# Rotation phasors made by ScalarE's sine beside the first down product, and a reshaped 1/rms step, in a two-layer FoX + S5 trunk

## The chip, the cores and the metric

The kernel runs on one core of a Trainium2 chip. The metric is the device time of one execution, in microseconds (us).

## The reference

Two layers, each a token mixer and a dense SwiGLU, on 1024 tokens of width 1024 in float32; every mixer and every SwiGLU stands between two rmsnorms.

```python
for i in range(DEPTH):                       # 2 layers
    h = rmsnorm(x, mix_pre_gain[i])
    m = fox_mixer(...) if i == 0 else s5_mixer(...)
    x = x + rmsnorm(m, mix_post_gain[i])
    h = rmsnorm(x, ffn_pre_gain[i])
    x = x + rmsnorm((silu(h @ w_gate) * (h @ w_up)) @ w_down, ffn_post_gain[i])

# s5_mixer: 64 groups of 64 complex states, 16 channels each
u = h @ w_in
a = exp((lam_re + 1j * lam_im) * dt)         # the pole of each state
bb = (a - 1) / lam * b
x_t = a * x_(t-1) + bb @ u_t                 # scan over the tokens
y = gelu(Re(c @ x_t) + d * u)
return (y * sigmoid(y @ w_glu)) @ w_out
```

`rmsnorm` is `x * rsqrt(mean(x^2) + eps) * gain`. What the change works on is the unit phasor of a pole, `exp(1j * angle * n)` for n = 0 to 127 tokens: the S5 stage turns its states by it.

## The kernel before, in words

Every product runs on TensorE in pieces of 128x512 from operands cut into a high and a low part (`split`: a cast on ScalarE, a subtraction on VectorE), three matmuls for one. SBUF is handed out as numbered pages: a ring such as `s5w0` or `s5w1` is one or more pages, and a tile's first write waits until the page's last user is done. The code fixes the order in which each engine gets its work through a scheduler, and all loads and stores go through SyncE's queue (SP) one behind the other.

The stages are, by the trace: first norm and start, attention (to about 600 us), its output product, `gate_up` 0 (775 to 1230), `down` 0 (1230 to 1415), the S5 mixer and its products (to 1806), `gate_up` 1 (to 2216), `down` 1, and the tail of the last norms.

`gate_up` has 11 periods p of 14 steps s. A step is 12 matmuls of 128x512. Beside the products of layer 0 a generator, `s5_params`, prepares the S5 mixer; the caller lets it go on by one piece after the steps (p, s) that `when` names: (5, 9, 12) in most periods. It begins with `s5_small` (poles, their powers, power tables), and then goes through 8 chunks of the states, one a period, the last after step 5 of the last period. In a chunk, before the change:

- GpSimd (POOL) makes `kg` and `cp` (L1183 to L1187); `kg` lies in ring `s5w1`. `cp_d` is stored (L1197).
- After step 5, TensorE multiplies `cp` into 16 small products `pk` (L1201); ScalarE copies them to `KT`, stored by L1207; POOL makes `bp` by L1237 to L1239, the lines of `prod`, which VectorE uses too.
- After step 9, `finish` transposes `bp` on TensorE (L1168, 8 matmuls of 128x128), copies it to `T` in ring `s5w1` (L1170) and stores it (`T_d`, L1171).
- Between steps 9 and 12, `s5_rot` multiplies two tables of phasors (`R1`: steps of 8, `R2`: steps of 1 or of 128) into the chunk's 128x1024 phasors `rot`, by six VectorE operations of 128x512 (`prod` again), in rings `s5w0` and `s5w1`. After step 12 they are stored (`rot_d`, L1228), and the next chunk's `kg` begins.

In the last period the steps are (5, 7, 9, 11). `down` multiplies the stored activations by the down weights in three phases of 11 steps; loads of both come through SP, and the casts for them run on ScalarE and VectorE. `rstd` (L301 to L304) makes 1/rms of 128 tokens from a sum of squares by a square root on ScalarE, a reciprocal and one refinement step on 128x1 values; `norm` applies it on VectorE (L314) or on POOL (L311, a multiplication by the gain, then L312, a scaling), and `to_fm` transposes the result on TensorE (L322).

Of the kernel before, what the change touches and what calls it, by code (L numbers as in the profile page):

```python
# [20 lines left out]
NF = FF // P  # L21
# [4 lines left out]
MAGIC = 1.5 * 2.0 ** 23  # L26
# [132 lines left out]
class Trunk:  # L159
# [129 lines left out]
    def rstd(self, src, junk, part=None, out=None):  # L289

        nc = self.nc
        V = nc.vector
        ss = self.small("ss")
        s = slice(0 if part is None else 512, D)
        nc.scalar.activation(junk[:, s], src[:, s], AF.Square, accum_out=ss)
        if part is not None:
            V.tensor_add(ss, ss, part)
        rt = self.small("rt")
        self.sqrt = nc.scalar.activation(rt, ss, AF.Sqrt, bias=self.eps, scale=1.0 / D)
        v, t, rr = self.small("vv"), self.small("tt"), self.small("rr") if out is None else out  # L300
        V.tensor_scalar(v, ss, -0.5 / D, -0.5 * EPS, op0=ALU.mult, op1=ALU.add)  # L301
        V.reciprocal(rr, rt)
        V.scalar_tensor_tensor(t, rr, v, rr, op0=ALU.mult, op1=ALU.mult)
        V.scalar_tensor_tensor(rr, t, 1.5, rr, op0=ALU.add, op1=ALU.mult)  # L304
        return rr

    def norm(self, src, gain, out, pool=False):
        nc = self.nc
        rr = self.rstd(src, out)
        if pool:  # L310
            nc.gpsimd.tensor_mul(out, src, gain)  # L311
            self.poolop = nc.gpsimd.tensor_scalar(out, out, rr, 1.0, op0=ALU.mult, op1=ALU.mult)  # L312
        else:
            nc.vector.scalar_tensor_tensor(out, src, rr, gain, op0=ALU.mult, op1=ALU.mult)  # L314
# [608 lines left out]

    def down(self, finish, begin=lambda tb, m: None, extra=0, last=3):

# [3 lines left out]
        nc, R = self.nc, self.R  # L929
# [11 lines left out]
        for ph in range(3):  # L941
            for p in range(n):
                g = self.take()
                if ph:
                    self.take()
                w = self.take()
                for tb in range(4):
                    mm(X[tb], g, w, 0, tb, p == ph == 0)
                    mm(Y[tb], g, w, 1, tb, p == 0)
                if ph == 0 and p < extra:  # L950
                    self.take()
            with self.tc.high_priority(AHEAD):
                for tb in range(4):
# [50 lines left out]
    def s5_small(self):  # L1004
# [48 lines left out]
        V.memset(hpi, math.pi / 2)  # L1053
        ang, n, r, sn, cs = (w[:, 8 + 3 * i:11 + 3 * i] for i in range(5))
        used[0] = 23
        for i, k in enumerate((1.0, 8.0, 128.0)):
            V.tensor_scalar_mul(ang[:, i], th, k)
        C1 = 6.28125
        C2 = math.floor((2 * math.pi - C1) * 2 ** 20) / 2 ** 20
        C3 = 2 * math.pi - C1 - C2  # L1060
        ts(n, ang, 1.0 / (2 * math.pi), MAGIC, op0=ALU.mult, op1=ALU.add)
        V.tensor_scalar_sub(n, n, MAGIC)
        for k, (x, o) in zip((C1, C2, C3), ((ang, r), (r, r), (r, r))):
            stt(o, n, -k, x, op0=ALU.mult, op1=ALU.add)
        ts(r, r, 3.1415925, -3.1415925, op0=ALU.min, op1=ALU.max)
        nc.scalar.activation(sn, r, AF.Sin)
        nc.scalar.activation(cs, r, AF.Abs)
        nc.scalar.activation(cs, cs, AF.Sin, bias=hpi, scale=-1.0)
        pw = R("pw", (P, 2, 9, 32))
        Pre, Pim = pw[:, 0], pw[:, 1]  # L1070
        self.R1, R2 = R("R1", (P, 2, 32, 16)), R("R2", (P, 1024))
        self.bs = R2[:, 512:640].rearrange("p (q g m) -> p q g m", q=4, g=2)
# [3 lines left out]
        nc.sync.dma_start(self.g5, bass.AP(tensor=v.tensor, offset=v.offset, ap=[[1, P], [P, 8]]))  # L1076
        self.R2 = R2[:, 0:512].rearrange("p (i a n) -> p i a n", i=2, n=8)
        R1, R2 = (x.rearrange("p i a n -> p i n a") for x in (self.R1, self.R2))
        for X in (pw, R1, R2):
            V.memset(X[:, 0, 0], 1.0)  # L1080
            V.memset(X[:, 1, 0], 0.0)
        tt(Pre[:, 1], mag, cs[:, 0], op=ALU.mult)
        tt(Pim[:, 1], mag, sn[:, 0], op=ALU.mult)
        for X, i in ((R1, 1), (R2, 2)):
            V.tensor_copy(X[:, 0, 1], cs[:, i])
            V.tensor_copy(X[:, 1, 1], sn[:, i])
        kk = R("s5t2", (P, 2, 16, 32))
# [12 lines left out]
        yield  # L1100
        powers(R1, 15)
        yield
        powers(R2, 7)

# [24 lines left out]
    def s5_params(self):  # L1129
# [84 lines left out]
        finish(7, bp)  # L1214
        yield from self.s5_rot(7)

    def s5_rot(self, ch):

        R, sh, V = self.R, (P, 4, 8, 16), self.nc.vector
        pr = slice(4 * ch, 4 * ch + 4)  # L1220
        rot, k = R("s5w0", sh[:1] + (2,) + sh[1:]), R("s5w1", sh[:1] + (2,) + sh[1:])
        e1 = [self.R1[:, i, pr, None, :].to_broadcast(sh) for i in range(2)]
        e2 = [self.R2[:, i, pr, :, None].to_broadcast(sh) for i in range(2)]
        self.prod(V, rot[:, 0], e1[0], e2[0], e1[1], e2[1], ALU.subtract, k[:, 0])
        self.prod(V, rot[:, 1], e1[0], e2[1], e1[1], e2[0], ALU.add, k[:, 1])
        yield
        with self.tc.issue_after(self.sp.ins):
            self.nc.sync.dma_start(self.rot_d[ch], rot.rearrange("p i a b c -> p (i a b c)"))  # L1228

# [268 lines left out]
def trunk(ctx: ExitStack, tc: tile.TileContext, A, out):  # L1498
# [179 lines left out]
```

## Time and profile before

| | |
|---|---|
| three runs | 2443.24, 2446.89 (the median), 2448.79 us |
| the profiled execution | 2441.36 us by its own time, span 2439.6 us |
| TensorE busy | 2362.7 us, 97% of the span |
| VectorE busy | 1747.5 us, 72% |
| ScalarE busy | 1175.4 us, 48% |
| POOL busy | 472.3 us, 19% |
| DMA | 318.25 MB, 130 GB/s in the mean |

The span is the time from the first to the last recorded instruction; the profiled execution's own time is 1.8 us longer, and it is 5.5 us under the median of the three. "Busy" counts the time in which an engine has an instruction at work. TensorE is busy but for 77 us, so what the profile lists as TensorE's waits is all that a change of order can win, except where the granted clock falls.

### The profile page before, as it was taken

The numbers are of one execution on the slowest core, as the hardware profiler recorded it, in microseconds if no ns is written. First come the engines' busy times: TensorE is split into PE (matmuls) and PEld (weight loads), VectorE is DVE, ScalarE is ACT, GpSimd is POOL, SyncE is SP. The second block draws the span as 40 slices with busy tenths as digits, with TensorE's granted clock in tenths as the row PEclk, the third lists the DMA queues.
The fourth block names the chain that finished last, engine by engine and source line by source line (L and its number), as shares of the span: only waits on it lengthen the run. The fifth ranks groups of instructions, "written<-read, shape, count | busy, mean of one in ns | idle before, by whom it ended". The sixth has DMA issues, their size and how long they took to land.

```text
span 2439.6 us, 31625 instructions
## 1 busy us (share of the span) xinstructions
PE 2362.7 (97%) x11683; PEld 1938.0 (79%) x11683; DVE 1747.5 (72%) x2746; ACT 1175.4 (48%) x1997; POOL 472.3 (19%) x427
## 2 busy tenths in 40 slices
PE   7999999999999999999999999999999999999998
PEld 5777778777777887777788888988878888888886
DVE  6867776677678968788678686763785656555867
ACT  5766676667646333433344363332453333333334
POOL 3222222223300035555530001320000000000003
PEclk9999999999999999999999999999999999999999
DMA  4221111121343433434498652443424233237874
GB/s 129 64 61 46 51 52 61 53 61 53 92 151 106 128 105 130 137 123 140 167 321 305 220 179 78 131 156 107 129 93 132 94 112 108 91 117 255 285 236 160
DMA packets 252428, 318.25 MB, mean 130 GB/s; under 512 B 34224, under 2 KB 179936, under 8 KB 252272
## 3 DMA queue, kind: packets, MB, share of 16 engines
q1 hardware_dynamic: 252272, 316.23, 40.1%
q8 instruction: 91, 1.49, 0.3%
q14 instruction: 65, 0.53, 0.1%
HBM read 238.46 MB, written 77.72 MB: 130 GB/s over the span
## 4 chain that ended last, share of the span: by engine, by line
PE 72%; DVE 12%; ACT 6%; POOL 4%; issue 3%; DMA 2%; SPq 0%; DVEq 0%; POOLq 0%; ACTq 0%
PE ps L837 27%; PE ps L939 15%; PE ps L272 7%; PE ps L274 7%; PE ps L273 7%; PE ps L584 2%; PE ps L603 2%; POOL s5w L1238 1%; DVE ps L551 1%; POOL s5w L1239 1%; DMA raw<-in_ffn_w_gate_dram 1%; ACT wh L253 1%; POOL s5w L1237 1%; PE ps L548 1%; PE ps L547 1%
## 5 line engine op out<-in xcount | busy, mean ns | idle before, releaser
L837 PE MATMUL ps<-B,ah 128*128 128x512 f32 x1056 | 327.3, 391 | 0.3 <-ACT B L89 0.2
L939 PE MATMUL ps<-wdh,gl 128*128 128x512 f32 x616 | 240.5, 391 | 1.8 <-DVE gl L254 1.8
L939 PE MATMUL ps<-wdl,gh 128*128 128x512 f32 x616 | 240.8, 391 | 0.6 <-DVE wdl L254 0.6
L939 PE MATMUL ps<-wdh,gh 128*128 128x512 f32 x616 | 240.3, 390 | 0.0
L837 PEld LDWEIGHTS ps<-B,ah 128*128 128x128 f32 x1056 | 197.6, 188 | 42.1 <-ACT B L89 1.2
L837 PE MATMUL ps<-ops,ah 128*128 128x512 f32 x704 | 220.1, 394 | 0.0
L272 PE MATMUL ps<-hT,wh 128*128 128x512 f32 x512 | 207.7, 406 | 1.2 <-DVE pt L425 0.6
L837 PE MATMUL ps<-B,al 128*128 128x512 f32 x528 | 205.5, 389 | 0.0
L273 PE MATMUL ps<-hT,wh 128*128 128x512 f32 x512 | 204.1, 399 | 0.0
L274 PE MATMUL ps<-hT,wl 128*128 128x512 f32 x512 | 202.5, 395 | 0.0
L253 ACT CAST gh<-gr 128x1024 fp32r<-128x1024 f32 (+1 forms) x78 | 81.2, 1041 | 206.0 <-PE ps L939 172.7
L588 DVE TENSOR_TENSOR ptl<-ps,pth 128x512 fp32r<-128x512 f32 x192 | 106.3, 554 | 78.7 <-ACT pth L587 73.7
L254 DVE TENSOR_TENSOR gl<-gr,gh 128x1024 fp32r<-128x1024 f32 (+1 forms) x78 | 98.3, 1262 | 88.2 <-ACT gh L253 88.2
L837 PEld LDWEIGHTS ps<-ops,ah 128*128 128x128 f32 x704 | 132.4, 189 | 29.3 <-issue 1.7
L1629 POOL TENSOR_TENSOR y<-m,s 128x512 f32<-128x512 f32 x4 | 7.2, 1796 | 764.8 <-DVE wdl L254 759.9
L543 POOL TENSOR_TENSOR An<-An,cmask 128x128 f32<-128x128 f32 x128 | 80.5, 630 | 367.2 <-DVE mx L551 332.7
L808 DVE TENSOR_TENSOR al<-raw,ah 128x1024 fp32r<-128x1024 f32 x88 | 111.8, 1272 | 44.8 <-ACT ah L807 44.7
L807 ACT CAST ah<-raw 128x1024 fp32r<-128x1024 f32 x88 | 92.3, 1050 | 99.2 <-PE ps L837 96.4
L837 PE MATMUL ps<-ops,al 128*128 128x512 f32 x352 | 137.8, 391 | 0.0
L939 PEld LDWEIGHTS ps<-wdh,gl 128*128 128x128 f32 x616 | 116.1, 188 | 26.4 <-DVE gl L254 2.4
L939 PEld LDWEIGHTS ps<-wdl,gh 128*128 128x128 f32 x616 | 116.1, 188 | 25.2 <-DVE wdl L254 1.3
L939 PEld LDWEIGHTS ps<-wdh,gh 128*128 128x128 f32 x616 | 116.0, 188 | 24.6 <-DVE s L862 0.5
(353 smaller groups left out, 5919.6 us busy)
## 6 DMA issues: line engine op xcount, KB each, us to landing
raw<-in_ffn_w_down_dram SPq DMA_DIRECT2D x98, 512.0 KB, 5.1
gr<-g_d SPq DMA_DIRECT2D x76, 512.0 KB, 4.3
raw<-in_ffn_w_gate_dram SPq DMA_DIRECT2D x44, 512.0 KB, 4.1
raw<-in_ffn_w_up_dram SPq DMA_DIRECT2D x44, 512.0 KB, 4.1
g_d<-s SPq DMA_DIRECT2D x66, 256.0 KB, 2.1
raw<-in_fox_w_in_dram SPq DMA_DIRECT2D x32, 512.0 KB, 4.2
g_d<-up SPq DMA_DIRECT2D x22, 512.0 KB, 2.6
g_d<-up SPq DMA_DIRECT2D x44, 256.0 KB, 2.4
```

The source lines that it names most:

```text
L253: self.nc.scalar.copy(h, src)
L254: self.lsub.tensor_sub(l, src, f32(h))
L272: mm(ps, lh, rh, start=start, stop=False)
L273: mm(ps, lh, rl, start=False, stop=False)
L274: mm(ps, ll, rh, start=False, stop=stop)
L543: nc.gpsimd.tensor_add(An[h][:, qs], An[h][:, qs], self.cmask)
L584: nc.tensor.transpose(p2[:, i], p[:, (g + i) * P:(g + i + 1) * P], self.ident)
L588: nc.vector.tensor_sub(dl, p2[:, 0:n], f32(dh))
L807: nc.scalar.copy(h, src)
L808: V.tensor_sub(l, src, f32(h))
L837: nc.tensor.matmul(bank, x[:, k], y, start=start and k == i == 0, stop=True, skip_group_check=True)
L939: nc.tensor.matmul(bank, x[:, j, t], y[:, j], start=start and i == 0, stop=True, skip_group_check=True)
```

## The change

It has three parts.

1. `rstd`: the two refinement operations took two SBUF tensors each (`scalar_tensor_tensor`). Now each takes one tensor, and the second value enters as a per-partition scalar (`tensor_scalar`).
2. The first norm: for token blocks 1 and 3 the gain multiplication on POOL is issued ahead of `rstd`, whose squares now go to a page of their own (`j`); the ring of `y` has one more page.
3. The phasors: the tables `R1` and `R2` go. `s5_small` makes a table `ph` of phases instead (sums of two phases, each brought back into one turn by subtraction). `s5_rot` leaves `s5_params`; it is run beside `down` 0, one half of a chunk after each of 8 steps in phase 0 and 8 in phase 2. A chunk is now one VectorE addition (128x512), an absolute value on ScalarE twice (128x512), once more and then the sine on both halves (128x1024), and the store. `s5_params` is called after steps (5, 12) in most periods, the last among them, and after 12 also in the second.

```diff
-        V.scalar_tensor_tensor(t, rr, v, rr, op0=ALU.mult, op1=ALU.mult)
-        V.scalar_tensor_tensor(rr, t, 1.5, rr, op0=ALU.add, op1=ALU.mult)
+        V.tensor_scalar(t, v, rr, rr, op0=ALU.mult, op1=ALU.mult)
+        V.tensor_scalar(rr, t, 1.5, rr, op0=ALU.add, op1=ALU.mult)
...
-    def norm(self, src, gain, out, pool=False):
+    def norm(self, src, gain, out, pool=False, junk=None):
+
         nc = self.nc
-        rr = self.rstd(src, out)
+        if junk is not None:
+            nc.gpsimd.tensor_mul(out, src, gain)
+        rr = self.rstd(src, out if junk is None else junk)
         if pool:
-            nc.gpsimd.tensor_mul(out, src, gain)
+            if junk is None:
+                nc.gpsimd.tensor_mul(out, src, gain)
...
-    def down(self, finish, begin=lambda tb, m: None, extra=0, last=3):
+    def down(self, finish, begin=lambda tb, m: None, beside=iter(()), steps=((),) * 3, extra=0, last=3):
...
+                if p in steps[ph]:
+                    next(beside, None)
...
-        nc.scalar.activation(sn, r, AF.Sin)
-        nc.scalar.activation(cs, r, AF.Abs)
+        nc.scalar.activation(sn, r[:, 0], AF.Sin)
+        nc.scalar.activation(cs, r[:, 0], AF.Abs)
...
-        powers(R1, 15)
-        yield
-        powers(R2, 7)
+        n, N = 1, kk.rearrange("p i n a -> p (i n a)").rearrange("p (n m) -> p n m", m=64)
+        while n < 15:
+            c_ = min(n, 15 - n)
+            x, q = X[:, n + 1:n + 1 + c_], N[:, :c_]
+            tt(x, X[:, 1:1 + c_], X[:, n:n + 1].to_broadcast([P, c_, 64]), op=ALU.add)
+            ts(q, x, 1.0 / (2 * math.pi), MAGIC, op0=ALU.mult, op1=ALU.add)
+            V.tensor_scalar_sub(q, q, MAGIC)
+            stt(x, q, -C1, x, op0=ALU.mult, op1=ALU.add)
+            stt(x, q, C1 - 2 * math.pi, x, op0=ALU.mult, op1=ALU.add)
+            ts(x, x, LIM, -LIM, op0=ALU.min, op1=ALU.max)
+            n += c_
+            if n == 8:
+                yield
...
                 finish(ch - 1, bp)
-                yield from self.s5_rot(ch - 1)
...
-        yield from self.s5_rot(7)
-
-    def s5_rot(self, ch):
...
+    def s5_rot(self):
+
+
+        act, sh = self.nc.scalar.activation, (P, 4, 8, 16)
+        mpi, hpi = self.mpi[:, 0:1], self.mpi[:, 1:2]
+        for ch in range(8):
+            pr = slice(4 * ch, 4 * ch + 4)
+            x, y = self.R("rx", sh), self.R("ry", (P, 2) + sh[1:])
+            with self.tc.high_priority(-150):
+                self.nc.vector.tensor_tensor(x, self.ph[:, 0, pr, None, :].to_broadcast(sh),
+                                             self.ph[:, 1, pr, 0:8, None].to_broadcast(sh), op=ALU.add)
+                act(y[:, 0], x, AF.Abs)
+                act(y[:, 1], x, AF.Abs, bias=hpi)
+            yield
+            with self.tc.high_priority(-150):
+                act(y, y, AF.Abs, bias=mpi)
+                act(y, y, AF.Sin, bias=hpi)
+            with self.tc.issue_after(self.sp.ins):
+                self.nc.sync.dma_start(self.rot_d[ch], y.rearrange("p i a b c -> p (i a b c)"))
+            yield
...
-            T.norm(xs[tb], g0[0], ys[tb], tb % 2 == 1)
+            T.norm(xs[tb], g0[0], ys[tb], tb % 2 == 1, R("j") if tb in (1, 3) else None)
...
-    first = {0: (8, 10, 12), 1: (5, 6, 8, 9, 10), NF // 2 - 1: (5, 7, 9, 11)}
+    first = {0: (8, 10, 12), 1: (5, 6, 8, 9, 10, 12)}
...
-    gu = T.gate_up(B, g_d[0], T.s5_params(), lambda p, s: s in first.get(p, (5, 9, 12)))
+    gu = T.gate_up(B, g_d[0], T.s5_params(), lambda p, s: s in first.get(p, (5, 12)))
...
-    T.down(fin0, extra=8)
+    T.down(fin0, beside=T.s5_rot(), steps=(range(3, 11), (), (0, 1, 3, 4, 6, 7, 9, 10)), extra=8)
```

On TensorE, in a middle period of `gate_up` 0, the transposes of `bp` stand before the change behind a step whose moving operand is `ah` and `al`, step 9 of the period (steps are counted from 0):

```order
L837 MATMUL ps<-ops_7027,ah_9626 128x512
L837 MATMUL ps<-ops_7025,al_9627 128x512
L1168 MATMUL ps<-ident,s5w_988_9603 128x128 x8
L837 MATMUL ps<-B_6067,ah_9552 128x512 x2
L837 MATMUL ps<-B_6067,al_9553 128x512
```

In the changed kernel they stand between the last two steps, which use the single operands `a`:

```order
L841 MATMUL ps<-ops_7054,a_976_9505 128x512
L841 MATMUL ps<-ops_7052,a_976_9505 128x512
L1187 MATMUL ps<-ident,s5w_980_9539 128x128 x8
L841 MATMUL ps<-ops_7051,a_984_9579 128x512
L841 MATMUL ps<-ops_7053,a_984_9579 128x512
```

They have moved from behind step 9 to behind step 12, by 36 matmuls of 128x512; the 16 products of `pk` have stayed after step 5.

On SP, the queue around the store of `T` in one period of `gate_up` 0 was this (`raw` are weights that come in, `g_d` the activations that go out):

```order
L899 DMA g_d<-s_8562 128x512
L1171 DMA T_d<-s5w_901_8766 128x1024
L1228 DMA rot_d<-s5w_902_8769 128x1024
L900 DMA g_d<-up_8563 128x1024
L904 DMA g_d<-s_8562 128x512
L905 DMA g_d<-up_8564 128x512
L906 DMA g_d<-up_8564 128x512
L231 DMA raw_8958<-in_ffn_w_gate_dram 128x8x128
L1197 DMA cp_d<-s5w_909_8835 128x1024
L231 DMA raw_9032<-in_ffn_w_up_dram 128x8x128
```

and is now this:

```order
L903 DMA g_d<-s_8525 128x512
L904 DMA g_d<-up_8526 128x1024
L1190 DMA T_d<-s5w_904_8786 128x1024
L908 DMA g_d<-s_8525 128x512
L909 DMA g_d<-up_8527 128x512
L910 DMA g_d<-up_8527 128x512
L231 DMA raw_8912<-in_ffn_w_gate_dram 128x8x128
L231 DMA raw_8986<-in_ffn_w_up_dram 128x8x128
L1215 DMA cp_d<-s5w_905_8789 128x1024
```

The phasors' store has left the period, `T_d` stands later, and both weight loads stand ahead of `cp_d`.

On ScalarE, where `gate_up` 0 ends (its last `silu` is the line `s<-ps`, L858 before and L862 now) and `down` 0 begins, before:

```order
L253 CAST gh_10470<-gr_10438 128x1024
L858 ACTIVATE s_10101<-s_10101 128x512
L858 ACTIVATE s_10102<-ps 128x512
L1342 CAST hT_10394<-raw_10474 128x512
L1342 CAST hT_10396<-raw_10474 128x512
L253 CAST gh_10428<-gr_10311 128x1024
L253 CAST wdh_10518<-raw_10486 128x1024
```

and now (L1245 to L1250 are the phasors of the first two chunks, L1189 is the copy of the last `T`):

```order
L253 CAST gh_10379<-gr_10347 128x1024
L862 ACTIVATE s_10019<-s_10019 128x512
L1245 ACTIVATE ry_10470<-rx_10469 128x512
L1246 ACTIVATE ry_10470<-rx_10469,mpi 128x512
L1249 ACTIVATE ry_10470<-ry_10470,mpi 128x1024
L1245 ACTIVATE ry_10562<-rx_10561 128x512
L1250 ACTIVATE ry_10470<-ry_10470,mpi 128x1024
L862 ACTIVATE s_10020<-ps 128x512
L1246 ACTIVATE ry_10562<-rx_10561,mpi 128x512
L1189 COPY s5w_1047_10266<-ps 128x1024
L1367 CAST hT_10303<-raw_10383 128x512
L1367 CAST hT_10305<-raw_10383 128x512
```

The first two chunks of phasors have moved ahead of and around the last `silu`, with the copy of the last `T` behind it.

## Rows read from the trace of the kernel before

**Rows 1.** The page's parts 1 and 2: span, busy time by engine.

```profile
span 2439.6 us, 31625 instructions
PE 2362.7 (97%) x11683; PEld 1938.0 (79%) x11683; DVE 1747.5 (72%) x2746; ACT 1175.4 (48%) x1997; POOL 472.3 (19%) x427
```

**Rows 2.** TensorE's waits: line <- releaser: total us, times, longest us.

```profile
PE ps L1168 <- POOL s5w L1239: 13.5, 8, 4.4
PE ps L322 <- DVE y L314: 11.8, 3, 8.2
...
PE ps L322 <- POOL y L312: 3.9, 2, 2.8
...
PE ps L837 <- DVE al L808: 3.3, 6, 0.6
...
PE ps L939 <- DVE gl L254: 1.8, 1, 1.8
```

**Rows 3.** Timeline of TensorE: start us, duration us, line, xcount, [idle before <- releaser].

```profile
999.55 0.98 PE L1168 MATMUL ps<-ident,s5w 128*128 128x128 f32 x7 [1.35 <-POOL s5w L1239]
...
1005.82 5.60 PE L837 MATMUL ps<-ops,a 128*128 128x512 f32 x24
1011.26 0.61 PE L837 MATMUL ps<-B,ah 128*128 128x512 f32 x2
...
1210.56 0.69 PE L1168 MATMUL ps<-ident,s5w 128*128 128x128 f32 x2 [4.37 <-POOL s5w L1239]
```

**Rows 4.** Windows: stretch, length, busy PE, PEld, DVE, ACT, POOL, clock, DMA.

```profile
1208.00:1212.00 4.00, 1.33 (x4) 0.82 (x5) 0.00 (x0) 0.00 (x0) 3.73 (x4) 0.71 0.76 296
1212.00:1216.00 4.00, 4.00 (x13) 3.42 (x13) 1.29 (x2) 1.96 (x2) 0.00 (x0) 0.50 0.19 72
1216.00:1220.00 4.00, 4.00 (x18) 3.21 (x18) 2.61 (x3) 2.21 (x3) 0.00 (x0) 0.93 0.74 221
```

**Rows 5.** Timeline of SP's queue, one period: issues of T, phasors, weights.

```profile
1001.90 0.38 SPq L1171 DMA_DIRECT2D T_d<-s5w  x1
1008.42 0.32 SPq L1228 DMA_DIRECT2D rot_d<-s5w  x1
...
1019.45 0.39 SPq L231 DMA_DIRECT2D raw<-in_ffn_w_gate_dram  x1
```

**Rows 6.** Timeline of POOL, the same period.

```profile
1008.53 1.44 POOL L1183 TENSOR_TENSOR s5w<-cc,pw 128x512 f32<-128x512 f32 x1 [8.17 <-DVE s5w L1239]
...
1018.54 3.32 POOL L1187 TENSOR_TENSOR s5w<-s5w 64x512 f32<-64x512 f32 x2
1029.81 1.56 POOL L1237 TENSOR_TENSOR s5w<-bb,pw 128x512 f32<-128x512 f32 x1 [7.95 <-PE ps L1201]
```

**Rows 7.** DMA issues: line, count, KB each, us to landing.

```profile
T_d<-s5w SPq DMA_DIRECT2D x8, 512.0 KB, 2.9
```

**Rows 8.** Timeline of VectorE, one of the six operations on phasors.

```profile
1006.51 0.69 DVE L1239 TENSOR_TENSOR s5w<-s5w,s5w 128x512 f32<-128x512 f32 x1
```

**Rows 9.** Groups of ScalarE by line: busy us, mean ns, idle before.

```profile
L858 ACT ACTIVATE s<-s 128x512 f32<-128x512 f32 x66 | 41.6, 630 | 122.2 <-DVE s L880 74.5 <-DVE s L873 41.6 <-DVE s L883 6.0
L295 ACT ACTIVATE fj<-m 128x1024 f32<-128x1024 f32 x16 | 16.9, 1054 | 11.1 <-DVE m L1596 11.1
```

**Rows 10.** Windows, columns as in 4: `s5_small`, then down 0.

```profile
815.00:858.00 43.00, 43.00 (x190) 35.41 (x190) 41.66 (x117) 16.53 (x28) 0.00 (x0) 1.00 0.41 117
...
1250.00:1300.00 50.00, 50.00 (x222) 41.45 (x221) 39.01 (x42) 24.47 (x29) 9.88 (x6) 1.00 0.90 324
```

**Rows 11.** Durations by line (ns, min/median/max) and two rows of VectorE's timeline.

```profile
L301 DVE TENSOR_SCALAR vv<-ss x64: 134/153/156, 5.8 to 2434.3; 128x1 f32<-128x1 f32 x64
...
L303 DVE SCALAR_TENSOR_TENSOR tt<-rr,vv x56: 205/219/2367, 6.3 to 2434.8; 128x1 f32<-128x1 f32 x56
...
9.54 1.89 DVE L303 SCALAR_TENSOR_TENSOR tt<-rr,vv 128x1 f32<-128x1 f32 x1
...
2397.00 2.49 DVE L254 TENSOR_TENSOR wdl<-raw,wdh 128x1024 fp32r<-128x1024 f32 x1
```

More of the change, by code (lines that the diff above doesn't have):

```diff
@@ L1053, in s5_small @@
         V.memset(hpi, math.pi / 2)
-        ang, n, r, sn, cs = (w[:, 8 + 3 * i:11 + 3 * i] for i in range(5))
-        used[0] = 23
+        ang, n, r = (w[:, 8 + 3 * i:11 + 3 * i] for i in range(3))
+        sn, cs = w[:, 17], w[:, 18]
+        used[0] = 19
         for i, k in enumerate((1.0, 8.0, 128.0)):
@@ L1060, in s5_small @@
         C3 = 2 * math.pi - C1 - C2
+        LIM = 3.141592
         ts(n, ang, 1.0 / (2 * math.pi), MAGIC, op0=ALU.mult, op1=ALU.add)
@@ L1064, in s5_small @@
             stt(o, n, -k, x, op0=ALU.mult, op1=ALU.add)
-        ts(r, r, 3.1415925, -3.1415925, op0=ALU.min, op1=ALU.max)
-        nc.scalar.activation(sn, r, AF.Sin)
-        nc.scalar.activation(cs, r, AF.Abs)
+        ts(r, r, LIM, -LIM, op0=ALU.min, op1=ALU.max)
+        nc.scalar.activation(sn, r[:, 0], AF.Sin)
+        nc.scalar.activation(cs, r[:, 0], AF.Abs)
         nc.scalar.activation(cs, cs, AF.Sin, bias=hpi, scale=-1.0)
@@ L1070, in s5_small @@
         Pre, Pim = pw[:, 0], pw[:, 1]
-        self.R1, R2 = R("R1", (P, 2, 32, 16)), R("R2", (P, 1024))
+        self.ph, R2 = R("R1", (P, 2, 32, 16)), R("R2", (P, 1024))
         self.bs = R2[:, 512:640].rearrange("p (q g m) -> p q g m", q=4, g=2)
@@ L1076, in s5_small @@
         nc.sync.dma_start(self.g5, bass.AP(tensor=v.tensor, offset=v.offset, ap=[[1, P], [P, 8]]))
[L1077 to L1086, printed above, removed]
+        V.memset(Pre[:, 0], 1.0)
+        V.memset(Pim[:, 0], 0.0)
+        tt(Pre[:, 1], mag, cs, op=ALU.mult)
+        tt(Pim[:, 1], mag, sn, op=ALU.mult)
+        X = self.ph.rearrange("p i a n -> p n (i a)")
+        V.memset(X[:, 0], 0.0)
+        V.tensor_copy(X[:, 1], r[:, 1:3].rearrange("p i a -> p (i a)"))
+        self.mpi = c.tile([P, 2], F32, name="mpi")
+        V.memset(self.mpi[:, 0:1], -math.pi)
+        V.memset(self.mpi[:, 1:2], -math.pi / 2)
         kk = R("s5t2", (P, 2, 16, 32))
@@ L1214, in s5_params @@
         finish(7, bp)
-        yield from self.s5_rot(7)
-    def s5_rot(self, ch):
[L1219 to L1228, printed above, removed]
+    def s5_rot(self):
[16 more added lines that the diff above has]
+            yield
     def pwr(self, i, o, pr):
@@ L1554, in trunk @@
     R.set(**{f"p{i}": [i] for i in [*range(7, 15), 35]}, vt=rg(15, 19), pth=rg(19, 22), ptl=rg(22, 25), pt=rg(25, 29) + [23, 24], An=[29, 30], Pt=[31, 32], RI=[36, 37],
-          o=[33, 34], x=[15, 16, 17, 18, 22, 13], y=[30, 12, 14], gn=[33], wf=[34], wr=[32], fg=[19, 20, 21])
+          o=[33, 34], x=[15, 16, 17, 18, 22, 13], y=[30, 12, 14, 31], gn=[33], wf=[34], wr=[32], fg=[19, 20, 21])
     x0 = A["x"][0]
@@ L1566, in trunk @@
     xs, ys = {}, {}
+    R.set(j=[36, 37])
     for tb in range(8):
@@ L1603, in trunk @@
     T.slots = (0, 2)
-    R.set(t=[15, 16], gh=[9, 37, 3], gl=[10, 36, 18], wdh=[11, 12, 35, 28], wdl=[13, 5, 29, 32], m=rg(19, 27), s=[27])
-    T.down(fin0, extra=8)
+    R.set(t=[15, 16], gh=[9, 37, 3], gl=[10, 36, 18], wdh=[11, 12, 35, 28], wdl=[13, 5, 29, 32], m=rg(19, 27), s=[27], rx=[4], ry=[33, 34])
+    T.down(fin0, beside=T.s5_rot(), steps=(range(3, 11), (), (0, 1, 3, 4, 6, 7, 9, 10)), extra=8)
     T.U = [R("U", (P, 8, 8, 16)) for _ in range(8)]
```

## The prediction

> **What bounds the kernel now.** I read the busy times first: TensorE works for 2362.7 of 2439.6 us [rows 1]. It is the bound in nearly every stage, and an edit that shortens other engines' work is worth only what it takes out of TensorE's 77 idle us, plus what TensorE loses at the lower clock. So the second view is the list of TensorE's waits [rows 2]. The largest entry, 13.5 us in 8 waits, is the transposes of `bp` waiting for POOL. Of the 11.8 + 3.9 us of the first norm's transposes, 8.2 us is the first input's way in, which no part of the change touches. 3.3 us in 6 waits is `gate_up` waiting for `al`; 1.8 us lies in the tail. The third view is the timeline. One `bp` wait in a middle period took 1.35 us, that of the last period 4.37 us [rows 3]. Behind the long one the granted clock fell: 0.71 in the window that holds the wait, 0.50 (1.2 GHz in place of 2.4) in the next, then 0.93 [rows 4].
>
> **The unit.** 24 matmuls of 128x512 run from 1005.82 to 1011.26 [rows 3]: 0.227 us each, 2.72 us for a step of 12.
>
> **The `bp` wait (the largest term).** POOL begins `bp` when the `pk` products are done and needs until a little behind step 9. Moving the transposes from behind step 9 to behind step 12 gives POOL 3 x 2.72 = 8.2 us more, against a wait of 1.35 us. In the last period they move from behind step 7 to behind step 12, 5 x 2.72 = 13.6 us, against 4.37. Every one of the 8 waits should vanish: -13.5 us. The transposes themselves (0.98 us for seven) stay. With the long wait goes the low clock behind it: from 1210.56 to 1212 half of 1.44 us is lost, then half of 4 us, then 0.07 of 4 us, 0.7 + 2.0 + 0.3 = 3.0 us. **Sum -16.5 us.** Below, a gain of 0 would need `bp` to come over 6.8 us later than now, which the next step bounds.
>
> **What the move makes late.** `T` lies in the page that the next chunk's `kg` needs, so `kg` now waits for the store of `T`. Before, `kg` waited for the phasors' last operation on VectorE, after 8.17 us of idle POOL (page release at 1008.53) [rows 6]; that release goes. From the end of step 12: transposes 1.1 us; from their end at 1000.53 to the issue of `T_d` at 1001.90 it took 1.4 us [rows 3, 5]; landing 2.9 us [rows 7]. `kg` can start at 5.4. `kg` and `cp` took from 1008.53 to 1018.54 + 3.32, 13.3 us [rows 6], so `cp` is ready at 18.7. `pk` is wanted seven steps later, behind step 5: 1.1 + 7 x 2.72 = 20.1 us. That leaves 1.4 us. I take no wait; the other end, with each of landing, issue and POOL a little later, is a wait of 1 us in each of 7 periods, +7. Here the two orders matter: on SP `T_d` stands behind one activation store, which may be late itself.
>
> **The `al` waits.** In the period shown, the load of the next gate weights was issued at 1019.45, behind stores of `up` that VectorE makes late [rows 5]. VectorE's six phasor operations at 0.69 us, 4.1 us a chunk [rows 8], and one store leave the period ahead of that load, and `cp_d` now stands behind both weight loads. I take -3.0 of the 3.3 us; the ends are 0 and -3.3.
>
> **`s5_small`.** The power tables of phasors give way to four rounds of sums and range reduction, about as many VectorE operations. In the stretch in which these run TensorE was busy 43.00 of 43.00 us with VectorE at 41.66 [rows 10], so neither order costs or gives: 0. If that cover were gone, each microsecond by which the last tables come late would count once.
>
> **`down` 0.** Each chunk brings one VectorE addition, 0.69 us by the nearest row, and on ScalarE two operations of 128x512 and two of 128x1024: 2 x 0.63 + 2 x 1.05 = 3.4 us by the rows of `silu` and of a square [rows 9]; 8 chunks make 27 us on ScalarE and 5.5 on VectorE. No row shows an absolute value or a sine of this size. The stage is 185 us long; in a window of 50 us ScalarE works 24.5 and VectorE 39.0 [rows 10], so there is room for 6 chunks' worth. The stores are the tighter part: 8 x 512 KB = 4.2 MB at 324 GB/s is 13 us of transfers, half of it in phase 0, where the DMA engines are 0.90 busy [rows 10]. That phase lasts about 60 us and has 6 us idle; 6.5 are wanted. And the stores stand in the same queue as the loads. I take +0.7 us: a load once or twice comes late. The ends are 0 and +6, the whole of phase 0's share in the open. At the change of stage the last `silu` has five phasor operations ahead of it, 0.63 x 3 + 1.05 x 2 = 4.0 us. It waits for the product of step 12, one step (2.72 us) ahead of `down`, and the bank it reads is wanted by `down`'s 13th matmul, another 12 x 0.227 = 2.7 us on: 5.4 us of room, so I put this at nothing too (in the open it would be those 4 us, once).
>
> **1/rms.** The refinement's first operation takes 219 ns in the median but 2367 at worst; that at 9.54 took 1.89 us. The one-tensor operation just ahead, L301, never took more than 156 ns in 64 [rows 11]. The long ones fall where POOL has a two-tensor operation at work. So the new form should not stall. But an operation on two tensors that comes next does, as L254 did for 2.49 us at 2397.00 [rows 11]: part of what is won moves on. At the start the waits behind the first are 11.8 + 3.9 - 8.2 = 7.5 us [rows 2]; with POOL's multiplication issued earlier as well, I take a sixth, -1.3 (ends 0 and -3). In the tail I take half of the 1.8 us wait [rows 2] and 0.07 us (219 less 153 ns) for each of the last four norms, which run one behind the other: -1.2 (ends 0 and -2.4). Elsewhere VectorE is not what ends last: 0.
>
> The Trainium skill, on the page "SBUF — State Buffer", section "Who interferes with whom", says that VectorE and GpSimd lock each other out when the VectorE operation has two SBUF inputs while GpSimd reads SBUF, for the whole instruction; rows 11 agree, with 2.49 us for L254. The same section says that `tensor_scalar` can enter a mode that takes the shared ports too. By that rule the new form would stall as the old one did and both terms for 1/rms would be 0, the sum 2.5 us less; L301, a `tensor_scalar` of the same size, speaks against it with 156 ns at most.
>
> **Sum.** -16.5 - 3.0 + 0.7 - 1.3 - 1.2 = -21.3 us. Against the profiled execution, 2441.36 - 21.3 = 2420.1. That execution is 5.5 us under the median of three (2446.89); by the median, 2425.6. I say **2425 us**. With the ends of the small terms alone (`al` 0 to -3.3, `down` 0 to +4, 1/rms 0 to -5.4) the likeliest case reaches from 2446.89 - 25.2 = 2422 to 2446.89 - 12.5 = 2434, and runs of one kernel differ by 3 us to either side.
>
> **Rivals.**
> 1. *`cp` comes late.* `kg` behind the store of `T` leaves 1.4 us. For it: POOL was 13.3 us at work there, with VectorE beside it, and the store has one more transfer ahead. Against it: VectorE has 4.1 us less to do, which should shorten POOL. Price 1 us in 7 periods: 2425 + 7 = 2432; with 2 us in each, 2439.
> 2. *The stall moves on.* The freed VectorE meets the same POOL operation one instruction later, or the one-tensor form stalls as well: the start and the tail stay. 2425 + 2.5 = 2428.
> 3. *Slower: the stores of phasors hold up SP's queue in `down` 0.* Each store waits in the queue for a sine, and loads behind it wait with it. If a sine is late, TensorE waits at each of 8 chunks. Over 21.3 / 8 = 2.7 us per chunk the whole gain is gone; at 3.5 us, 2425 + 28 = 2453. For it: 0.90 DMA share. Against it: ScalarE is half idle, and TensorE never stood still in these 50 us (50.00) [rows 10].
> 4. *The transposes still wait.* POOL's chain slips with the schedule, so that `bp` is again just too late behind step 12. It would take 6.8 us; only the clock and the last wait would be won: 2446.89 - 4.4 - 3.0 = 2439.5, or with a late chain in the last period too, no change at 2445.
>
> **Chances.** The forecast 0.62, rival 1 0.15, rival 2 0.13, rival 3 0.05, rival 4 0.05. A measurement of this kernel tells no change from about 0.2%, 4.9 us. Faster: forecast, rivals 1 and 2 and part of 4, 0.92; the same 0.04; slower 0.04. The range 2415 to 2437 takes the likeliest case with the scatter of runs to both sides, rival 2 and most of rival 1; what it leaves out is rivals 3 and 4 and the far end of 1.
>
> **What the profile would show.** Right: no wait of TensorE for `bp` (13.5 us now); a granted clock of 1.00 through 1205 to 1225; `gate_up` 0 shorter by 16 to 20 us; refinement operations never over 0.25 us; TensorE without gaps in `down` 0. The step on `T` shows in POOL's idle time ahead of `kg`, which should end with the store of `T`, and in TensorE's waits at `pk`, which should be under 1 us in all. Wrong: waits at `pk` of 1 us and more in each period (rival 1); L314 or L254 stalled by over 2 us at the start and in the tail (rival 2); gaps at L939's successor in `down` 0 that end with a load (rival 3); waits ahead of the transposes (rival 4).

## The result and the profile after

The changed kernel takes 2427.26 us in the median of 4 runs (2423.86 to 2428.97), the one before 2447.84 (2443.24 to 2449.52): 20.6 us less, a ratio of 0.9903 with an interval of 0.9873 to 0.9932. The profiled execution took 2426.33 us by its own time; against that of before (2441.36, faster than all four) it is 15.0 us less. Where these 15 us come from is read from the traces; that the medians differ by 5.6 us more is a matter of which execution of before was profiled.

Span and busy time by engine after the change (front of the page), which answer to [rows 1]:

```profile
span 2424.5 us, 31559 instructions
PE 2359.3 (97%) x11683; PEld 1938.8 (80%) x11683; DVE 1689.1 (70%) x2684; ACT 1204.4 (50%) x2029; POOL 455.2 (19%) x427
```

TensorE's waits after the change (line <- releaser: total us, times, longest), which answer to [rows 2]:

```profile
PE ps L326 <- DVE y L318: 9.6, 2, 8.2
...
PE ps L943 <- ACT m L962: 3.7, 1, 3.7
PE ps L326 <- POOL y L316: 3.3, 2, 2.2
...
PE ps L943 <- DVE gl L254: 1.9, 2, 1.2
...
PE ps L943 <- ACT m L965: 1.8, 1, 1.8
...
PE ps L943 <- DVE wdl L254: 0.8, 1, 0.8
```

The transposes of `bp` and the `al` operands have left the list: 13.5 and 3.3 us before, nothing now. Two entries are new, `down` waiting for L962 and L965, the copies of finished banks on ScalarE. The windows of `gate_up` 0 (columns as in [rows 4]) show TensorE without a gap for 421 us and at the full clock to the end:

```profile
775.00:1196.00 421.00, 421.00 (x1975) 346.24 (x1974) 306.16 (x440) 173.93 (x265) 173.33 (x129) 1.00 0.41 127
1196.00:1230.00 34.00, 33.74 (x152) 27.43 (x151) 23.32 (x21) 24.50 (x32) 16.67 (x10) 1.00 0.88 284
```

First and last starts of TensorE's lines (xcount, ns min/median/max, first to last start) show the rest:

```profile
L943 PE MATMUL ps<-wdh,gh x616: 387/389/797, 1203.0 to 2414.0; 128*128 128x512 f32 x154
L272 PE MATMUL ps<-woh,wh x256: 387/389/504, 652.2 to 1772.2; 128*128 128x512 f32 x128
L272 PE MATMUL ps<-hT,ih x192: 277/283/501, 1424.6 to 1562.2; 128*128 128x256 f32 x128, 128*128 128x512 f32 x64
```

| start of | before | after | stage before it |
|---|---|---|---|
| out_proj 0 (L272, `woh`) | 654.9 | 652.2 | start and attention: -2.7 |
| `down` 0 (L939, now L943) | 1230.2 | 1203.0 | out_proj 0 and `gate_up` 0: -24.5 |
| S5 input product (L272, `ih`) | 1441.6 | 1424.6 | `down` 0: **+10.2** |
| last `down` matmul of this form | 2429.8 | 2414.0 | S5 to `down` 1: +1.2 |
| end of the span | 2439.6 | 2424.5 | tail: +0.7 |

So `gate_up` 0 gave more than forecast (out_proj 0 lasts 120.1 us in both), and `down` 0 took back 10 us: 5.8 us of waits, 3.7 and 1.8 of them at its two changes of phase, and 4.2 us more of busy time (215.5 us against 211.3). There TensorE stood still at the first change of phase, and the clock fell behind it:

```profile
1264.00:1268.00 4.00, 0.43 (x1) 0.43 (x2) 3.36 (x6) 2.48 (x3) 0.00 (x0) 0.84 1.00 357
1268.00:1272.00 4.00, 3.89 (x9) 2.55 (x9) 4.00 (x6) 3.29 (x5) 0.00 (x0) 0.50 0.82 295
1272.00:1276.00 4.00, 4.00 (x16) 3.23 (x15) 4.00 (x6) 1.21 (x2) 0.00 (x0) 0.81 0.92 346
```

ScalarE's timeline of the same place (start, us, line; in brackets the idle time and what ended it):

```profile
1259.02 0.61 ACT L1245 ACTIVATE ry<-rx 128x512 f32<-128x512 f32 x1
1259.54 0.71 ACT L1246 ACTIVATE ry<-rx,mpi 128x512 f32<-128x512 f32 x1
1260.28 1.15 ACT L1249 ACTIVATE ry<-ry,mpi 128x1024 f32<-128x1024 f32 x1
1261.34 1.03 ACT L253 CAST gh<-gr 128x1024 fp32r<-128x1024 f32 x1
1262.27 1.15 ACT L1250 ACTIVATE ry<-ry,mpi 128x1024 f32<-128x1024 f32 x1
1265.04 1.05 ACT L253 CAST wdh<-t 128x1024 fp32r<-128x1024 f32 x1 [1.62 <-DVE t L761]
1265.99 1.04 ACT L253 CAST gh<-gr 128x1024 fp32r<-128x1024 f32 x1
1266.94 0.58 ACT L962 COPY m<-ps 128x512 f32<-128x512 f32 x1
1268.71 1.04 ACT L253 CAST wdh<-t 128x1024 fp32r<-128x1024 f32 x1 [1.19 <-DVE t L761]
1269.66 1.55 ACT L962 COPY m<-ps 128x512 f32<-128x512 f32 x3
```

The bank copies stand behind casts of a weight sum `t` that is late, and those behind a chunk of phasors. ScalarE also waits for the store of a page that it is to write again:

```profile
ACT ry L1245 <- DMA rot_d<-ry: 18.2, 3, 7.1
```

### The profile page after: what moved, and what is told of

Same layout as the page of the kernel before. It is cut to its first block, busy times and chain, and to the rows that moved or that the text cites. A ratio compares the mean times of both kernels' runs of the same rounds, so it can differ in the third digit from the quotient of the medians.

```text
span 2424.5 us, 31559 instructions
## 1 busy us (share of the span) xinstructions
PE 2359.3 (97%) x11683; PEld 1938.8 (80%) x11683; DVE 1689.1 (70%) x2684; ACT 1204.4 (50%) x2029; POOL 455.2 (19%) x427
## 4 chain that ended last, share of the span: by engine, by line
PE 74%; DVE 12%; ACT 7%; DMA 3%; issue 3%; POOL 0%; SPq 0%; DVEq 0%; ACTq 0%; POOLq 0%
PE ps L841 33%; PE ps L943 10%; PE ps L272 7%; PE ps L274 7%; PE ps L273 7%; PE ps L588 2%; PE ps L607 2%; DVE ps L555 1%; DMA raw<-in_ffn_w_down_dram 1%; DMA rot_d<-ry 1%; ACT wh L253 1%; PE ps L552 1%; PE ps L551 1%; DVE ptl L592 1%; DVE y L318 1%
## 5 line engine op out<-in xcount | busy, mean ns | idle before, releaser
L943 PE MATMUL ps<-wdh,gh 128*128 128x512 f32 x616 | 241.4, 392 | 6.3 <-ACT m L962 3.7
L943 PE MATMUL ps<-wdh,gl 128*128 128x512 f32 x616 | 240.9, 391 | 1.9 <-DVE gl L254 1.9
L943 PE MATMUL ps<-wdl,gh 128*128 128x512 f32 x616 | 240.9, 391 | 0.8 <-DVE wdl L254 0.8
L272 PE MATMUL ps<-hT,wh 128*128 128x512 f32 x512 | 207.5, 406 | 1.3 <-DVE pt L429 0.7
L812 DVE TENSOR_TENSOR al<-raw,ah 128x1024 fp32r<-128x1024 f32 x88 | 117.1, 1333 | 50.5 <-ACT ah L811 50.5
L943 PEld LDWEIGHTS ps<-wdh,gh 128*128 128x128 f32 x616 | 116.3, 189 | 32.8 <-ACT m L962 4.2
L943 PEld LDWEIGHTS ps<-wdh,gl 128*128 128x128 f32 x616 | 116.2, 189 | 26.9 <-DVE gl L254 2.7
L943 PEld LDWEIGHTS ps<-wdl,gh 128*128 128x128 f32 x616 | 116.3, 189 | 25.5 <-DVE wdl L254 1.5
```

The source lines that it names most:

```text
L272: mm(ps, lh, rh, start=start, stop=False)
L812: V.tensor_sub(l, src, f32(h))
L943: nc.tensor.matmul(bank, x[:, j, t], y[:, j], start=start and i == 0, stop=True, skip_group_check=True)
```

## The experiments

**What in `down` 0 costs the 10 us?** Four kernels, compared with the kernel before on one chip (the changed kernel did not run on that chip; it took 2427.3 and 2427.5 us in two other series). The first takes the phasors out of `down` 0 (the S5 stage then reads the phase table).

```diff
-    T.down(fin0, beside=T.s5_rot(), steps=...
+    T.down(fin0, steps=...
             nc.sync.dma_start(self.T_d[ch], T)
+            nc.sync.dma_start(self.rot_d[ch], self.ph.rearrange("p i a n -> p (i a n)"))
```

> Leaves out the making of the phasors beside down 0; the 512 KB store of each chunk is made in gate_up 0 instead, from the phase table (so the S5 stage turns its states by wrong numbers, at the same cost). The changed kernel's down 0 is about 10 us longer than that of the kernel before, from the first matmul of down to the first of the S5 input product. All theories: that stretch falls from 221.6 to about 211 us, and the time from 2427 to about 2417 us. If it stays at 2427, the loss is not the phasors'.

2419.8 us, ratio 0.9893 (0.9877 to 0.9909); `down` 0 lasts 1202.9 to 1419.2, 216.3 us against 221.6. Half of the 10 us in that one execution, 7.5 by the medians (about 211 us and 2417 us were expected). At the changes of phase TensorE doesn't wait at all here. What is left, 4.9 us against before, has another cause: two waits early in phase 0, for a down weight that is cast late, and a granted clock of 0.69 in the window of 1218 to 1222 behind them.

```profile
1215.56 0.49 PE L943 MATMUL ps<-wdh,gh 128*128 128x512 f32 x1 [0.98 <-ACT wdh L253]
1217.01 0.76 PE L943 MATMUL ps<-wdl,gh 128*128 128x512 f32 x1 [0.96 <-DVE wdl L254]
```

The changed kernel has no such wait in that place. So this run understates what the phasors cost; why that weight comes late without them stays open.

The second keeps the arithmetic and moves the stores as above.

```diff
             with self.tc.high_priority(-150):
                 act(y, y, AF.Abs, bias=mpi)
                 act(y, y, AF.Sin, bias=hpi)
-            with self.tc.issue_after(self.sp.ins):
-                self.nc.sync.dma_start(self.rot_d[ch], y...)
             yield
```

> The changed kernel with the phasors' arithmetic beside down 0 (VectorE and ScalarE) but with the stores moved to gate_up 0, made from the phase table (the arithmetic's result is not used). Theory A, ScalarE stands still because a phasor operation waits for the store of the page that it writes, and the copies of finished banks stand behind it: no store, no wait, 2417 to 2419 us. Theory B, the stores take transfer time from the loads: 2417 to 2419 as well. Theory C, the 3.4 us a chunk of ScalarE's own time delays the casts and copies: stays at 2425 to 2427 us.

2421.9 us, 0.9903 (0.9887 to 0.992), between the theories. The clock stays at 1.00, and one wait at the first change of phase is left, for L963, the addition on VectorE behind the bank copy:

```profile
PE ps L943 <- DVE m L963: 2.5, 1, 2.5
```

`down` 0 lasts 215.5 us, 4.1 more than before the change. So the arithmetic alone (theory C) does cost something at the change of phase, though less than half of the 10 us.

The third keeps the stores and leaves out the arithmetic.

```diff
-            x, y = self.R("rx", sh), self.R("ry", (P, 2) + sh[1:])
-            ... the addition, the absolute values and the sine ...
+                self.nc.sync.dma_start(self.rot_d[ch], self.ph...)
```

> The changed kernel with the eight stores beside down 0 in their places, but from the phase table and without the arithmetic (no VectorE addition, no absolute value, no sine). Theory A (waits on the store of the page to be written) and theory C (ScalarE's own time): 2417 to 2419 us. Theory B (transfers): stays at 2424 to 2427 us.

2420.2 us, 0.9896 (0.988 to 0.9912), like the first, with the same two early waits (0.9 and 1.0 us) and none at a change of phase: theory B falls as a cause by itself. The fourth gives the phasors a third page.

```diff
-    R.set(..., rx=[4], ry=[33, 34])
+    R.set(..., rx=[4], ry=[33, 34, 14])
```

> The changed kernel with three pages for the phasors in place of two, nothing else. Theory A: the 18 us in which ScalarE waits for a store of phasors go for the most part, and TensorE's waits of 3.7 and 1.8 us with them: 2418 to 2421 us. Theories B and C: 2425 to 2428 us.

2428.0 us, 0.9924 (0.9909 to 0.994): no gain. ScalarE's wait for a store is gone from its list, and yet TensorE waits at the change of phase:

```profile
PE ps L943 <- ACT m L962: 4.9, 1, 4.9
```

```profile
1264.79 1.05 ACT L253 CAST wdh<-t 128x1024 fp32r<-128x1024 f32 x1 [5.55 <-DVE t L761]
1265.75 1.05 ACT L253 CAST gh<-gr 128x1024 fp32r<-128x1024 f32 x1
1269.53 1.05 ACT L253 CAST wdh<-t 128x1024 fp32r<-128x1024 f32 x1 [2.73 <-DVE t L761]
1270.48 1.04 ACT L253 CAST gh<-gr 128x1024 fp32r<-128x1024 f32 x1
1271.42 1.55 ACT L962 COPY m<-ps 128x512 f32<-128x512 f32 x3
```

Theory A falls for the first change of phase; at the second, the wait of 1.8 us for L965 is gone in this run. ScalarE was idle for 5.55 and again for 2.73 us with the copies in its queue, behind casts whose input was late (the sums `t` themselves wait for loads of down weights, 2.05 us ahead of the first). The stores alone do nothing at the changes of phase, the arithmetic alone leaves 2.5 us, and both together use up the lead of loads and casts.

**Is it the phase, or the place ahead of a change of phase?**

```diff
-steps=(range(3, 11), (), (0, 1, 3, 4, 6, 7, 9, 10))
+steps=((), range(2, 10), range(1, 9))
```

> The changed kernel with the phasors' pieces called after steps 2 to 9 of phase 1 and 1 to 8 of phase 2 of down 0, and none in phase 0. Theory D, the loss needs both the stores and ScalarE's extra work in phase 0, where the DMA engines are 0.9 busy: without them there the wait of 3.7 us at the first change of phase and the low clock behind it go, 2419 to 2422 us. Rival, the loss moves with the phasors to the second change of phase: 2425 to 2430 us.

2426.4 us, 0.9939 (0.9926 to 0.9951, on a chip where the kernel before took 2439.5): the rival. The wait has gone to the second change of phase, 3.6 us for L965. The scheduler had moved chunks up to it: seven of the eight were made ahead of the copies there, where the steps ask for four. Here ScalarE did stand still for a store, as theory A has it:

```profile
1323.46 0.63 ACT L1245 ACTIVATE ry<-rx 128x512 f32<-128x512 f32 x1 [8.14 <-DMA rot_d<-ry]
```

So the next two hold the phasors behind the bank copies (`bc` is the last such copy) in place of the raised priority, and differ in the steps.

```diff
-            with self.tc.high_priority(-150):
+            with self.tc.issue_after((self.bc or self.sp).ins):
...
-                        nc.scalar.copy(a[:, lo], X[tb])
+                        self.bc = nc.scalar.copy(a[:, lo], X[tb])
...
-steps=(range(3, 11), (), (0, 1, 3, 4, 6, 7, 9, 10))
+steps=(range(0, 6), range(1, 7), range(1, 5))      # bc_h
+steps=(range(0, 6), (), range(0, 10))              # bc_j
```

> The changed kernel once more, beside the two below, so that they are compared on one chip: 20 us under the kernel before, as in its first runs, a ratio of 0.990 to 0.994.

> The changed kernel with the phasor operations on ScalarE and VectorE held behind the copies of finished banks: chunks 0 to 2 early in phase 0 of down 0, 3 to 5 right behind the copies at the first change of phase, 6 and 7 behind those at the second. Theory E, the loss comes from phasor operations in the steps ahead of a change of phase, where they use up the lead of loads and casts so that the bank copies stand behind a cast that waits: both waits (3.7 and 1.8 us) and the low clock go, 5 to 8 us under the changed kernel. Rival, the load on ScalarE and the DMA engines costs the same wherever it stands: within 2 us of the changed kernel.

> As the one before, with chunks 0 to 2 early in phase 0 and 3 to 7 behind the copies at the second change of phase, where the DMA engines were 0.6 to 0.7 busy before the change. Theory E: 5 to 8 us under the changed kernel, like the one before or a little more. Rival: five chunks in one phase crowd ScalarE (17 us more in 60) and make casts late in phase 2: within 3 us of the changed kernel.

The changed kernel again: 2427.5 us, 0.986 (0.9824 to 0.9895; the kernel before took 2459.0 on this chip, so the ratio is lower than expected). The two others: 2419.8 and 2418.3 us, both 0.9826 (0.9794 to 0.9858), 8 and 9 us under it. Theory E holds, as far as a run can say that changes the fence, the priority and the steps at once; which of them is needed was not parted. In the last one `down` 0 lasts from 1203.9 to 1415.8, 211.9 us, as before the change (211.4); this is the lowest median of the study, and all that TensorE waits for in `down` 0 and 1 is (both waits lie in `down` 1)

```profile
PE ps L944 <- DVE wdl L254: 0.8, 1, 0.8
PE ps L944 <- DVE gl L254: 0.8, 1, 0.8
```

**What gave the gain in `gate_up` 0?** The transposes go back behind step 9, the phasors stay out:

```diff
-    first = {0: (8, 10, 12), 1: (5, 6, 8, 9, 10, 12)}
+    first = {0: (8, 10, 12), 1: (5, 6, 8, 9, 10, 12), NF // 2 - 1: (5, 7)}
-... first.get(p, (5, 12))
+... first.get(p, (5, 9))
```

> The changed kernel with the transposes of bp back behind step 9 (behind step 7 in the last period) and the next chunk's kg right behind them; the phasors stay beside down 0. Theory S, the step number carries the gain in gate_up 0: the eight waits for bp return (13.5 us before) with the low clock of the last period (3 us), 2441 to 2446 us. Theory R, the gain comes from taking the phasors' six VectorE operations and their store out of the period, which lets POOL finish bp in time: the waits stay small, 2427 to 2432 us.

2464.0 us, ratio 1.0097 (1.0082 to 1.0113), slower than before the change; `down` 0 begins at 1241.0. The time is neither theory's. The waits for `bp` are 2.8 us in 3, only 0.2 of it outside the last period, as theory R had it: POOL finishes `bp` 12.2 to 12.9 us behind the start of `pk`, where it took 13.2 to 13.8 before the change. But there are these waits:

```profile
PE ps L841 <- DVE al L812: 12.7, 7, 2.6
...
PE ps L841 <- ACT ah L811: 4.0, 1, 4.0
```

And the granted clock falls behind the `al` wait in each of six periods, here behind 2.22 us at 1027.61:

```profile
1028.00:1032.00 4.00, 4.00 (x18) 2.66 (x18) 3.12 (x4) 0.97 (x3) 0.00 (x0) 0.57 0.15 55
```

`gate_up` 0 lasts 468.5 us in this run, 37.8 more than in the changed kernel: TensorE is idle for 20.6 us against 1.5 and busy for 447.9 against 429.2, at a mean granted clock of 0.96 against 1.00. So half of the loss is idle time and half is busy time that grew.

SP's queue and VectorE in one period of that kernel, then SP and VectorE in the same place of the changed kernel:

```profile
1020.46 0.39 SPq L231 DMA_DIRECT2D raw<-in_ffn_w_gate_dram  x1
...
1010.24 1.66 DVE L900 TENSOR_TENSOR up<-s,s 128x512 f32<-128x512 f32 x1
1011.82 1.77 DVE L901 TENSOR_TENSOR up<-s 128x512 f32<-128x512 f32 x1
```

```profile
1005.30 0.64 SPq L231 DMA_DIRECT2D raw<-in_ffn_w_gate_dram  x1
...
999.41 0.69 DVE L900 TENSOR_TENSOR up<-s,s 128x512 f32<-128x512 f32 x1
1000.02 0.68 DVE L901 TENSOR_TENSOR up<-s 128x512 f32<-128x512 f32 x1
```

With the transposes early, POOL's `kg` (from 1006.05) runs beside the additions on which the stores of `up` wait; they take 1.7 us in place of 0.7, and the weight load behind those stores goes out after `kg`. With the transposes behind step 12 the additions and the load are through before `kg` begins (1006.33). But the kernel before the change looks much the same as this slow one. At the same place of the period (step 12 begins at 1005.82 there, at 1005.74 here) its additions are as long, and its load goes out at 1019.45 [rows 5], 1.0 us earlier; there the matmul that waits for `al` lost 0.58 us, not 2.22, and the clock stayed at 1.00:

```profile
1010.97 1.60 DVE L896 TENSOR_TENSOR up<-s,s 128x512 f32<-128x512 f32 x1
1012.49 1.77 DVE L897 TENSOR_TENSOR up<-s 128x512 f32<-128x512 f32 x1
...
1026.05 0.51 PE L837 MATMUL ps<-T,al 128*128 128x512 f32 x1 [0.58 <-DVE al L808]
```

So a `kg` beside the additions does not by itself cost what this run lost; what the two differ by is 1.0 us of the load and the clock behind the wait. A last kernel was to part the two, `kg` one piece later than the transposes:

```diff
                 finish(ch - 1, bp)
+                yield
...
+... 2: (5, 12), NF // 2 - 1: (5, 9)} ... first.get(p, (5, 9, 12))
```

> The changed kernel with the transposes of bp behind step 9 in every period, the last among them, as in the run with both pieces moved, but with the next chunk's kg issued only behind step 12. That run had hardly any wait for bp (2.8 us) but waits for al of 12.7 us, and was the slowest of all. Theory K, what costs there is kg on POOL at the same time as VectorE's additions of the last steps, which makes the stores of up and the next weight load behind them late: with kg back behind step 12 the al waits go, and some wait for bp of 1 to 2 us in each of 8 periods may come back: 2428 to 2440 us. Rival, the place of the transposes themselves costs: al waits stay over 8 us, 2450 us and more.

2456.2 us, 0.998 (0.9963 to 0.9996), `al` waits of 13.7 us. But it did not move `kg`:

```profile
1005.43 1.60 POOL L1202 TENSOR_TENSOR s5w<-cc,pw 128x512 f32<-128x512 f32 x1 [5.77 <-DMA T_d<-s5w]
```

It starts with the landing of `T`, 6.8 us behind the start of the transposes (998.66), as in the run before. So this run doesn't tell the rival apart; that `kg` beside the additions makes the load late is read from the timelines, not shown by a run of its own.

**The two parts on 1/rms**, each undone alone:

```diff
-        V.tensor_scalar(t, v, rr, rr, op0=ALU.mult, op1=ALU.mult)
+        V.scalar_tensor_tensor(t, rr, v, rr, op0=ALU.mult, op1=ALU.mult)
(and the second operation in the same way: old_rstd)
-  ..., tb % 2 == 1, R("j") if tb in (1, 3) else None)
+  ..., tb % 2 == 1, None)                       (old_norm)
```

> The changed kernel with the two refinement operations of 1/rms on two SBUF tensors again. Theory of the prediction: the one-tensor form is worth 1.2 us in the tail and a part of the 1.3 us at the start, so 2428.5 to 2430 us. Rival: the stall has only moved to the next two-tensor operation (2.8 and 3.4 us in the tail's residual updates in the changed kernel's trace), and a pointer scalar makes each of the two operations 0.05 us longer: no difference beyond 1 us, 2426 to 2428.

> The changed kernel with the first norm's gain multiplication on POOL behind 1/rms again, as before the change. The three gaps of TensorE at the start that the changed kernel shows (2.18, 1.43, 1.15 us) were 2.81, 1.88, 1.04 and 1.67 before. If the early multiplication is what shortened them, the first gap returns to 2.8 and the time goes up by 0.6 to 2 us, 2428 to 2429; if the one-tensor refinement did it, nothing changes, 2427.

2432.1 us (more than either theory said; the runs reach from 2426.8 to 2435.7), 0.9964 (0.9951 to 0.9977), and 2427.0 us, 0.9944 (0.9932 to 0.9957), on the chip of the kernel with phases 1 and 2. The first product behind attention starts at 654.8 us with the old refinement, at 652.7 with the old order of the norm, at 652.2 with both changes (651.9 to 652.8 in the runs that have both): the one-tensor form is worth 2 to 3 us at the start, the early multiplication nothing that these runs can tell. From the last `down` matmul of the first form to the end of the span it took 10.1 us with the old refinement, 9.5 to 11.3 in the runs with the new one and 9.8 before the change: the tail gains nothing that can be told.

## Why the prediction was right, step by step

It said 2425 us, and 2427.26 was measured; two steps were off by several us and in opposite directions. Part of the closeness is luck. The forecast's terms sum to -21.3 us, the stages of the two traces to -15.1: `gate_up` 0 gave 5.0 more than forecast, `down` 0 took 9.5 more, and the rest was 1.7 worse. That the medians still differ by 20.6 comes from a profiled execution of before that was 6.5 us under its median.

- **The `bp` wait: right in mechanism, too small.** All eight waits went, and the clock stayed at 1.00. The step was needed: `bp` came 12.5 to 15.1 us behind the start of `pk`, in part because it now waits for the store of `cp` (19.0 us in 6 waits), which the forecast did not have. Forecast with `al`: -19.5; the trace: -24.5. In `gate_up` 0 TensorE's busy time fell as well, 437.0 to 429.2 us for the same matmuls. 3.0 us of these 7.8 were forecast as low clock. The transposes alone went from 11.3 to 8.3: 1.2 of it in the last period, where they ran at the low clock, and 0.26 in each of the other seven, where the wait had cut the row of eight in two (0.33 + 0.98 us before, 1.03 in one row now). So these interrupted rows cost more than the idle time that the list of waits names; the other 3 us were not taken apart.
- **`T` ahead of `kg`: right, and close.** POOL waits 12.35 us for `T_d` ahead of `kg`, as forecast, and TensorE doesn't wait at `pk`:

```profile
1006.33 1.11 POOL L1201 TENSOR_TENSOR s5w<-cc,pw 128x512 f32<-128x512 f32 x1 [12.35 <-DMA T_d<-s5w]
...
1013.99 3.85 POOL L1205 TENSOR_TENSOR s5w<-s5w 64x512 f32<-64x512 f32 x2
```

  `cp` was ready at 1017.84 and `pk` began at 1018.55, a margin of 0.7 us where 1.4 was forecast: the store landed in 3.9 us, not 2.9, and POOL took 11.5 us, not 13.3.
- **The `al` waits: right in size, wrong in cause.** They went, but not since the phasors left VectorE: without phasors, and with the transposes early, they were 12.7 us. By the timelines the place of `kg` against the last additions and the load decides; no run shows that by itself.
- **`s5_small`: right**, no gap. **The change of stage: right**, TensorE waited 0.3 us there (1.2 in the later run of the same kernel).
- **`down` 0 is the step that failed.** It was put at +0.7 us, with ends of 0 and +6. It was +10.2 in the profiled execution and 7.5 to 9 by the medians. The forecast compared ScalarE's and the DMA engines' spare time over the stage with the work added. The work was sized well (a chunk's four operations take 0.6 + 0.7 + 1.15 + 1.15 = 3.6 us on ScalarE, where 3.4 was estimated), and the stores alone are absorbed, as their run shows. But the spare time is no reserve at a change of phase, where bank copies stand in order behind casts that need late loads: the arithmetic alone left a wait of 2.5 us there, both together 3.7 and 1.8. Rival 3 had the stage, not the mechanism: TensorE did not wait at each chunk, but at two places, with some 3 us of low clock behind one.
- **1/rms.** The start gave 2.7, not 1.3; the tail nothing, not 1.2. The new operations are never stalled, but slower, not faster, than the old ones at their best (ns min/median/max):

```profile
L303 DVE TENSOR_SCALAR tt<-vv,rr x56: 259/272/275, 6.2 to 2419.7; 128x1 f32<-128x1 f32 x56
...
L304 DVE TENSOR_SCALAR rr<-tt,rr x56: 199/214/218, 6.5 to 2420.0; 128x1 f32<-128x1 f32 x56
```

  Medians before were 219 and 159: 0.1 us more for each norm of the serial end, where 0.07 less was forecast from L301, which has no pointer scalar. And in the tail the stall moved on, as rival 2 had it, to the residual update (POOL's L1668 is at work from 2386.72 for 3.39 us and from 2391.27 for 3.50):

```profile
2388.37 2.81 DVE L1671 SCALAR_TENSOR_TENSOR x<-y,rr,x 128x1024 f32<-128x1024 f32 x1
...
2392.43 3.43 DVE L1671 SCALAR_TENSOR_TENSOR x<-y,rr,x 128x1024 f32<-128x1024 f32 x1
```

  The rule of the Trainium skill, page "SBUF — State Buffer", section "Who interferes with whom", that `tensor_scalar` can enter a mode that takes the shared ports, did not bite at 128x1: 275 ns at most in 56, one of them at 2388.18 with POOL at work. Its other rule, on two SBUF inputs, agrees with these two rows (1.28 us when POOL is idle). With the old refinement back, no residual update took over 1.28 us, and L303 took up to 2.38 instead.

## What to carry to other kernels

Before moving work into a stage, look at the places where an engine's queue holds a release that TensorE needs (bank copies at a change of phase), and ask what stands ahead of it there; a mean busy share says nothing about them. Work that a scheduler may move up needs a fence behind such a place: holding the phasors behind the copies, with the steps chosen to suit, was worth 8 to 9 us. Moving a helper's piece by a few steps can be worth more than the wait that it removes: with the transposes put back, `gate_up` 0 lost 37.8 us, where the wait named for them had been 13.5. That the piece which follows the transposes causes it is likely, not shown.

## What was not expected of the hardware

- A 512 KB store took 4.9 to 8.1 us to land in `down` 0 (median 7.1), against 2.6 in the median in `gate_up` 0 before.
- A gap of 3.7 us in `down` 0 was followed by stretches at a granted clock of 0.50 and 0.81; one of 2.5 us in the run with the arithmetic alone by none below 1.00. Yet in the kernel with the transposes back behind step 9, gaps of 1.8 to 2.6 us, one in each of six periods, were each followed by a stretch at a lowered clock (0.57 in the window shown). The length of the gap alone doesn't tell.
- The kernel before took 2439.5 to 2461.1 us in the median of five series on at least four chips, the changed one 2427.3 and 2427.5 in two series. So the gain is 20.6 us in the first and 31.5 in the second; why the old kernel scatters more stays open.
